# Second projection of a feed-forward block by rows of tokens instead of by columns of features

## The chip, the cores and the metric

The kernel runs on one core of a Trainium2 chip. The metric is device time in microseconds (us) of one execution, from the first to the last instruction of the core and what lies around it. Five engines work side by side, each through its own queue, in order: PE (TensorE, matrix products; its weight loads are shown apart as PEld), DVE (VectorE), ACT (ScalarE), POOL (GpSimd) and SP (SyncE, which here issues most DMAs).

## The reference

One layer of a streaming encoder for 2048 prompt tokens and 64 sample tokens, in float32. A mixer (windowed attention and a gated MLP) gives `mix`; then

```
h = layernorm(ALPHA * x + mix) * ln1_g + ln1_b          # 2112 x 1024
gu = h @ w_gate_up                                      # 1024 x 5632
f = (silu(gu[:, :2816]) * gu[:, 2816:]) @ w_down        # 2816 x 1024
y = layernorm(ALPHA * h + f) * ln2_g + ln2_b            # returned
```

with ALPHA = 2 ** 0.25. The change lies in how `h` is left behind by the first norm and in the last two lines. The mixer is as it was, up to the output projection.

## The kernel before

**Products.** Each operand of a product is split into two rounded terms (`split`: ACT copies the rounded term, DVE or POOL subtracts it to get the rest), and a product is three matmuls, high by high, high by low and low by high (`mm3`, lines 146 to 148, and lines 754 to 756). In a matmul one operand of 128 columns is loaded into the array (the stationary one) and the other streams through it (the moving one); "128x264" in a profile row is the moving operand.

**Output projection and first norm** (lines 584 to 653). Tile by tile of 128 tokens (17 tiles, the last of 64): `m2_load`, `m2_split`, `m2_mm` (48 matmuls of 512 columns, PSUM name `po`), `m2_add`, `m2_ln` (the norm without gain and shift, on DVE), `m2_T` (eight transposes on PE, then ACT multiplies by `ln1_g` and adds `ln1_b`, which lie along the partitions now) and a DMA of `h` by features, transposed, to `h_d` in DRAM.

**Feed-forward.** The 2112 tokens are cut into four blocks of 528. In a block, for each of 22 tiles of the hidden dimension, gate and up projections take seven products of half a block's tokens instead of eight (Strassen's scheme; `product`, 12 matmuls of 264 columns each, PSUM names `accA`, `accB`, `accC`). The weights' sums are made on POOL (`sums`, and line 732), and each weight form is split by ACT and by DVE or POOL (`form`, PSUM-free, two SBUF operands, 512 columns). The block's activations are loaded and their sums made and split in `prep_steps`, around the end of the block ahead of it: eight subtractions on POOL (line 671), fourteen splits on DVE (`hf`).

**Second projection.** Every two hidden tiles, `down` adds their products to y. y is kept by features: `yT` is eight tiles of 128 features by 528 tokens. `w_down` is stationary, `ff` is moving, 264 tokens at a time, so a pair of hidden tiles takes 16 calls of six matmuls (PSUM name `pd`) and 16 additions on DVE (line 1097). At the end of a block each `yT` tile goes to DRAM (`spill_y`), and the next block's start value is loaded from `h_d` (`new_y`). In the middle of the next block `finish_steps` fetches y in pieces of 106 tokens (`yf`), turns them by transposes on PE (`yTp`, eight for a piece, 15 pieces), and does the last norm: statistics, `norm` on ACT, `gain` on DVE (two operations), `shift` on POOL (two operations), DMA out. In the last block `z_old` turns the five pieces from SBUF (40 transposes) and the last two hidden tiles are multiplied by rows (`z_mm`, PSUM name `zp`: here `ff` is stationary and 512 columns of `w_down` move).

**Order.** All of it is written out by hand. `order` lists the products, 154 to a block; a product's place in it is called a position here. `make` builds weight forms five positions ahead. `at(pos, f)` puts every other piece of work behind the product at a position. For a pair of hidden tiles c, `p0` is the position of the product 3 of its second tile; for a block's last pair, p0 is the block's last position. Each engine runs its part of this list in order.

Of the kernel before, what the change touches and what calls it, by code (L numbers as in the profile page):

```python
# [35 lines left out]
PARTS = [[(106 * i, min(106, TB - 106 * i)) for i in range(5)]] * 3 + [[(116 * i, min(116, TB - 116 * i)) for i in range(5)]]  # L36
# [7 lines left out]
def hybrid_step(ctx: ExitStack, tc: tile.TileContext, x_prompt, x_sample, xT_prompt, xT_sample, cache_kT, cache_v, w_in,  # L44
# [14 lines left out]
    dram = ctx.enter_context(tc.tile_pool(name="dram", bufs=1, space=DRAM))  # L59
    wpool = ExitStack()  # L60
# [3 lines left out]
    y_d = [dram.tile([P, KD, TB], F32, name=f"y_d{b}") for b in range(NB - 1)]  # L64
    h_d = [dram.tile([P, KD, TB], F32, name=f"h_d{b}") for b in range(NB)]
# [76 lines left out]
    def mm3(out, parts):  # L142
        """out = sum of a^T b over parts, each an exact sum of two rounded terms"""
# [15 lines left out]
    def go(f, *a):  # L159
        """the next part of a step of the mixer"""  # L160
# [15 lines left out]
    def split_v(t, src, m):  # L176
        """a tile's values: per group the rounded term, then the rest"""
# [8 lines left out]
    def do_B(t):  # L186
# [7 lines left out]
        # rotary embedding of the first 16 dimensions of each head  # L194
# [38 lines left out]
    def split_k(t, cols, src):  # L233
        """a tile's keys in two terms, each on both halves of the partitions"""
# [86 lines left out]
    def spans(t):  # L321
        """columns of the scores of the even and the odd chunk of a tile"""
# [80 lines left out]
    def dup_v(t):  # L403
        """the values of a tile's first chunk and of the second one before it, each on both halves of the partitions"""
# [6 lines left out]
    def attn_PV(t, g):  # L411
        """the values' two terms lie side by side, so that the products of both come at once"""
# [57 lines left out]
    # constants of the mixer  # L470
# [32 lines left out]
    # a row of the first chunk doesn't see the second  # L503
# [61 lines left out]
    # weights of the output projection  # L565
# [54 lines left out]
    def m2_ln(t):  # L620
# [9 lines left out]
        nc.vector.tensor_scalar(tt[:m], tt[:m], mv[:m, 0:1], rs[:m], op0=ALU.subtract, op1=ALU.mult)  # L630

    def m2_T(t):
# [5 lines left out]
        for h in range(2):  # L638
# [20 lines left out]
    def prep_steps(b):
        """steps that bring a block's activations, and their sums, into the products' operands"""  # L660
        t = {}

        def load(key, kk, kh, sh):
            t[key, kk] = f1.tile([P, 2, NH], F32, name="hraw", tag="hraw", bufs=4)
            k0 = 4 * kh + 2 * kk
            nc.sync.dma_start(out=t[key, kk], in_=h_d[b][:, k0:k0 + 2, sh * NH:(sh + 1) * NH])

        def sub(out, x, y, kk):
            if (out, kk) not in t:
                t[out, kk] = f1.tile([P, 2, NH], F32, name="hsum", tag="hsum", bufs=2)  # L670
            nc.gpsimd.tensor_tensor(out=t[out, kk], in0=t[x, kk], in1=t[y, kk], op=ALU.subtract)

        def put(prod, key, kk):
            if kk == 0:
                forms[b, prod] = f1.tile([P, 2, 4, NH], F32R, name=f"hf{prod}", tag=f"hf{prod}", bufs=1)
# [3 lines left out]
        # each step with the position before the end of the block ahead after which it may come  # L679
# [26 lines left out]
    def slab_piece():  # L706
        return f1.tile([P, 4, P], F32, name="wsum", tag="hraw", bufs=4)
# [717 lines left out]
```

## Time and profile before

| | us |
|---|---|
| median of 3 runs (2229.14 to 2234.25) | 2230.99 |
| span of the profiled execution | 2229.8 |
| PE busy in the span | 2123.0 |
| DVE, ACT, POOL busy | 1756.9, 1147.4, 1026.5 |

The profiled execution's time is its span and about 1.2 us around it, if it is taken as the median run. Matmuls overlap in the array, so a busy PE says only that one was under way; how fast they follow each other is read from their start times. In rows of a timeline the columns are start, duration (us), engine, line, operation, output and inputs, shape, count, and in brackets the engine's idle time ahead of it and what ended it. Rows of windows give the length of each stretch, then the busy time of each engine with its instructions, then the mean granted TensorE clock (1.00 is 2.4 GHz, 0.50 is 1.2 GHz), the DMA share and GB/s.

### The profile page before, as it was taken

Reading aid. Unit: us, or ns where it says so; the run is one execution under the profiler, and the core shown is the slowest. Engines: PE = TensorE matmul, PEld = TensorE weight load, DVE = VectorE, ACT = ScalarE, POOL = GpSimd, SP = SyncE. Lnnn points to the kernel's source line nnn. Section 1 sums busy time; section 2 is a strip of 40 time slices with the busy share of each in tenths; the row PEclk is TensorE's granted clock in tenths of the full one; section 3 lists DMA queues with packets and bytes.
Section 4 is the critical chain, followed back from the end, with each engine's and each line's share of the span. In section 5 each row is a group of like instructions: output and inputs, shape, how many; then the busy total and the mean of one; then the engine's idle time right before and its main releaser. Section 6 shows DMA issues by size and latency. Waiting matters only on the chain.

```text
span 2229.8 us, 40289 instructions
## 1 busy us (share of the span) xinstructions
PE 2123.0 (95%) x15307; PEld 1996.7 (90%) x15307; DVE 1756.9 (79%) x3511; ACT 1147.4 (51%) x2675; POOL 1026.5 (46%) x813
## 2 busy tenths in 40 slices
PE   8999999989998999998999999899999989999995
PEld 6888888868887999998998999899999989999994
DVE  6877777786777877778777887877788787778876
ACT  6666656565565444445444444444444444444443
POOL 0222222230114646456555665656565656556642
PEclk9999999989999999999999999999999999999998
DMA  5111111134545332333533333353243335333321
GB/s 194 39 39 39 39 39 44 37 125 154 190 135 168 101 105 91 105 119 101 168 105 114 113 111 112 120 163 115 91 136 93 121 116 161 114 99 125 106 77 39
DMA packets 134096, 237.60 MB, mean 107 GB/s; under 512 B 36334, under 2 KB 59118, under 8 KB 133902
## 3 DMA queue, kind: packets, MB, share of 16 engines
q1 hardware_dynamic: 112638, 225.00, 31.5%
q10 hardware_dynamic: 21088, 9.70, 1.6%
q8 instruction: 120, 1.97, 0.3%
q14 instruction: 74, 0.61, 0.1%
q0 software_dynamic: 176, 0.33, 0.0%
HBM read 202.22 MB, written 32.77 MB: 105 GB/s over the span
## 4 chain that ended last, share of the span: by engine, by line
PE 55%; DVE 28%; ACT 8%; DMA 4%; issue 4%; POOL 0%; SPq 0%; ACTq 0%; DVEq 0%; POOLq 0%
DVE wf L101 6%; PE accA L755 5%; PE pd L146 5%; PE pd L147 5%; PE accA L754 5%; PE pd L148 5%; PE accA L756 5%; DMA yf<-y_d 3%; DVE yT L1097 3%; PE po L146 3%; PE po L147 3%; PE po L148 3%; DVE wd L101 3%; PE accC L755 2%; PE accC L756 2%
## 5 line engine op out<-in xcount | busy, mean ns | idle before, releaser
L146 PE MATMUL pd<-ff,wd 128*128 128x264 f32 x1376 | 398.8, 290 | 26.8 <-DVE yT L1097 25.4
L754 PE MATMUL accA<-hf,wf 128*128 128x264 f32 x1408 | 403.6, 287 | 7.7 <-ACT a L760 6.0
L756 PE MATMUL accA<-hf,wf 128*128 128x264 f32 x1408 | 402.9, 286 | 3.1 <-POOL wf L101 2.0
L755 PE MATMUL accA<-hf,wf 128*128 128x264 f32 x1408 | 404.7, 287 | 0.0
L147 PE MATMUL pd<-ff,wd 128*128 128x264 f32 x1376 | 393.6, 286 | 0.4 <-DVE ff L101 0.4
L148 PE MATMUL pd<-ff,wd 128*128 128x264 f32 x1376 | 392.9, 286 | 0.0
L101 DVE TENSOR_TENSOR wf<-wsum,wf 128x512 fp32r<-128x512 f32 x351 | 302.5, 863 | 28.4 <-ACT wf L100 28.3
L732 POOL TENSOR_TENSOR wsum<-guraw,wsum 128x512 f32<-128x512 f32 x87 | 114.1, 1311 | 443.9 <-DVE wf L101 432.7
L101 POOL TENSOR_TENSOR wf<-guraw,wf 128x512 fp32r<-128x512 f32 x173 | 267.9, 1549 | 70.3 <-ACT wf L100 66.6
L1097 DVE TENSOR_TENSOR yT<-pd,yT 128x264 f32<-128x264 f32 x624 | 252.1, 422 | 56.1 <-PE pd L148 56.1
L146 PEld LDWEIGHTS pd<-ff,wd 128*128 128x128 f32 x1376 | 261.0, 190 | 34.7 <-DVE yT L1097 34.5
L754 PEld LDWEIGHTS accA<-hf,wf 128*128 128x128 f32 x1408 | 268.8, 191 | 8.9 <-ACT a L760 6.9
L723 POOL TENSOR_TENSOR wsum<-guraw 128x512 f32<-128x512 f32 x176 | 269.3, 1530 | 15.1 <-PE accA L756 7.0
L756 PEld LDWEIGHTS accA<-hf,wf 128*128 128x128 f32 x1408 | 268.4, 191 | 3.6 <-POOL wf L101 2.2
L755 PEld LDWEIGHTS accA<-hf,wf 128*128 128x128 f32 x1408 | 269.0, 191 | 0.0
L147 PEld LDWEIGHTS pd<-ff,wd 128*128 128x128 f32 x1376 | 260.6, 189 | 0.6 <-DVE ff L101 0.6
L148 PEld LDWEIGHTS pd<-ff,wd 128*128 128x128 f32 x1376 | 260.3, 189 | 0.0
L100 ACT CAST ff<-c 128x264 fp32r<-128x264 f32 x176 | 72.7, 413 | 312.4 <-DVE c L767 312.4
L101 DVE TENSOR_TENSOR wd<-draw,wd 128x512 fp32r<-128x512 f32 x176 | 201.0, 1145 | 25.0 <-ACT wd L100 22.7
L100 ACT CAST wf<-wsum 128x512 fp32r<-128x512 f32 x351 | 216.4, 617 | 0.7 <-POOL wsum L723 0.5
L755 PE MATMUL accC<-hf,wf 128*128 128x264 f32 x704 | 201.3, 286 | 1.8 <-DVE hf L101 1.8
L754 PE MATMUL accC<-hf,wf 128*128 128x264 f32 x704 | 200.1, 284 | 1.3 <-DVE c L779 1.3
(285 smaller groups left out, 5424.4 us busy)
## 6 DMA issues: line engine op xcount, KB each, us to landing
guraw<-in_w_gate_up_dram SPq DMA_DIRECT2D x176, 512.0 KB, 4.2
draw<-in_w_down_dram SPq DMA_DIRECT2D x176, 256.0 KB, 4.5
hraw<-h_d SPq DMA_DIRECT2D x32, 264.0 KB, 4.2
yT<-h_d SPq DMA_DIRECT2D x32, 264.0 KB, 2.7
x<-in_xT_prompt_dram SPq DMA_DIRECT2D x32, 256.0 KB, 4.4
catx<-cat_d SPq DMA_DIRECT2D x16, 512.0 KB, 3.6
catx<-in_x_prompt_dram SPq DMA_DIRECT2D x16, 512.0 KB, 5.9
h_d<-catx ACTq DMA_DIRECT2D x13, 512.0 KB
```

Of the source, the lines that this page charges most:

```text
L100: nc.scalar.copy(hi, src)
L101: (on or nc.vector).tensor_tensor(out=lo, in0=src, in1=hi.bitcast(F32), op=ALU.subtract)
L146: nc.tensor.matmul(out, ah, bh, start=(i == 0), stop=False)
L147: nc.tensor.matmul(out, ah, bl, start=False, stop=False)
L148: nc.tensor.matmul(out, al, bh, start=False, stop=(i == n - 1))
L723: nc.gpsimd.tensor_tensor(out=src[key], in0=src[x], in1=src[y], op=op)
L732: nc.gpsimd.tensor_tensor(out=s4, in0=gu_src[b, i][2], in1=src, op=ALU.subtract)
L754: nc.tensor.matmul(ps, wh, hh, start=(new and k == 0), stop=False, skip_group_check=not new)
L755: nc.tensor.matmul(ps, wh, hl, start=False, stop=False, skip_group_check=not new)
L756: nc.tensor.matmul(ps, wl, hh, start=False, stop=(k == 3), skip_group_check=not new)
L1097: nc.vector.tensor_tensor(out=y, in0=pd[:, :NH], in1=y, op=ALU.add)
```

## The change

The second projection is turned round. `ff` is stationary, 128 tokens at a time, and 512 columns of `w_down` move, so the products come out as rows of tokens. Blocks are 512, 512, 512 and 576 tokens, which are 4, 4, 4 and 5 whole tiles (the fifth has 64 tokens). y stays in SBUF as rows, five tiles of 128 by 1024; nothing of it goes to DRAM and back, and no transposes are left in the last norm. The start value is no longer read from `h_d`: `m2_ln` now applies gain and shift itself (both times ALPHA, spread over the partitions once by `m2_gains`), its rows go to DRAM as `hy_d`, and `m2_T`'s ACT step only takes ALPHA off again. The last norm of a block runs beside the last pair's products instead of in the middle of the next block. Buffers: weight forms 7 for 8, sums 3 for 4, raw `w_down` 3 for 4; the sum for product 7 is made later; products add in place; the second hidden tile's weights are loaded later, and the first tile's form 3 is built from its sources.

```diff
-TB = TOK // NB
-NH = TB // 2
+TB = (512, 512, 512, 576)
+TILES = tuple(tuple(range(4 * b, 4 * b + (5 if b == NB - 1 else 4))) for b in range(NB))
...
     def m2_ln(t):
...
-        nc.vector.tensor_scalar(tt[:m], tt[:m], mv[:m, 0:1], rs[:m], op0=ALU.subtract, op1=ALU.mult)
+        nc.vector.scalar_tensor_tensor(out=tt[:m], in0=tt[:m], scalar=mv[:m, 0:1], in1=gb_t[0][:m], op0=ALU.subtract, op1=ALU.mult)
+        nc.vector.scalar_tensor_tensor(out=tt[:m], in0=tt[:m], scalar=rs[:m], in1=gb_t[1][:m], op0=ALU.mult, op1=ALU.add)
+    def m2_gains():
+        for v in range(2):
+            gb_t[v] = f1.tile([P, KD, P], F32, name="gb", tag="raw", bufs=4).rearrange("p k q -> p (k q)")
+            for h in range(2):
+                pt = ps1.tile([P, 4, P], F32, name="gbp", tag="pj")
+                for j in range(4):
+                    c = 16 + 8 * v + 4 * h + j
+                    nc.tensor.transpose(pt[:, j], vecT[:, c:c + 1].to_broadcast([P, P]), ident)
+                nc.scalar.activation(gb_t[v][:, h * 512:(h + 1) * 512], pt.rearrange("p j q -> p (j q)"), AF.Copy, scale=ALPHA)
...
     def m2_T(t):
...
-            for j in range(4):
-                k = 4 * h + j
-                nc.scalar.activation(hT[:, k, :m], pt[:, j, :m], AF.Identity, scale=vecT[:, 16 + k:17 + k],
-                                     bias=vecT[:, 24 + k:25 + k])
+            nc.scalar.activation(hT[:, 4 * h:4 * h + 4, :m], pt[:, :, :m], AF.Copy, scale=1.0 / ALPHA)
...
+        nc.scalar.dma_start(out=h_d[b][:, :, o:o + m], in_=hT[:, :, :m])
+        nc.scalar.dma_start(out=hy_d[t][:m], in_=tt[:m])
...
-    m2_ln(0)
     go(gate_T, 16)
...
+    m2_gains()
     for t in range(NT - 4):
...
-        if t:
-            m2_ln(t)
+        m2_ln(t)
...
-        if t in (NT - 10, NT - 7):
-            load_gu(0, (t - NT + 10) // 3)
+        if t == NT - 10:
+            load_gu(0, 0)
...
     m2_ln(16)
-    make(EARLY)
+    load_gu(0, 1)
     product(*order[0])
...
-    def down(b, c, j, s):
+    def down(b, c, t, h, last=False):
...
-        mm3(pd[:, :NH], [((wd[b, i, j // 4][:, 0, js], wd[b, i, j // 4][:, 1, js]), (ff[b, i][:, 0, sl], ff[b, i][:, 1, sl]))
-                         for i in (2 * c, 2 * c + 1)])
+        mm3(pd[:m], [((ff[b, i][:, 0, o:o + m], ff[b, i][:, 1, o:o + m]), (wd[b, i, h][:, 0], wd[b, i, h][:, 1]))
+                     for i in (2 * c, 2 * c + 1)])
+        y = y_t[t][:m, h * 512:(h + 1) * 512]
+        nc.vector.tensor_tensor(out=y, in0=pd[:m], in1=y, op=ALU.add)
+    def new_y(t):
+        m = rows(t)
+        y_t[t] = f2.tile([P, D], F32, name="y", tag="y", bufs=5)
+        nc.sync.dma_start(out=y_t[t][:m], in_=hy_d[t][:m])
...
-        if b:
-            for k, e in enumerate(PARTS[b - 1]):
-                for q, f in enumerate(finish_steps(b - 1, *e)):
-                    at(first + (39, 53, 66, 81, 95)[k] + (0, 2, 3, 5, 5, 7, 7, 8)[q], f)
...
+            if c < NFF // 2 - 1:
+                where = (2, 3, 4, 5, 7, 8, 9, 10, 12, 13) if last else (2, 4, 5, 7, 9, 10, 12, 13)
+                for k, (h, t) in enumerate((h, t) for h in range(2) for t in TILES[b]):
+                    at(p0 + where[k], lambda b=b, c=c, t=t, h=h: down(b, c, t, h))
+            elif not last:
+                new = list(TILES[b + 1])
+                at(p0 + 3, lambda t=new.pop(0): new_y(t))
+                for k, t in enumerate(TILES[b]):
+                    for h in range(2):
+                        at(p0 + (6, 7, 8, 9, 10, 11, 12, 13)[2 * k + h], lambda b=b, c=c, t=t, h=h: down(b, c, t, h))
+                    steps = finish_steps(t)
+                    for q, f in zip((7, 8, 9, 10, 11), steps):
+                        at(p0 + 2 * k + q, f)
+                    at(p0 + 2 * k + 13, lambda t=new.pop(0): new_y(t)) if new else None
```

The five steps of `finish_steps(t)` are now: statistics of the first half; of the second half, and their moments (with the reciprocal root on POOL); `norm`, one ACT operation over 1024 columns; `gain`, two DVE operations; `shift`, two POOL operations and one DMA out. `z_mm` and what follows it keep their order and work on the rows in place.

## Rows read from the trace of the kernel before

**Rows 1.** The page's first part: busy time of the engines, share of the span, instructions.

```profile
PE 2123.0 (95%) x15307; PEld 1996.7 (90%) x15307; DVE 1756.9 (79%) x3511; ACT 1147.4 (51%) x2675; POOL 1026.5 (46%) x813
```

**Rows 2.** Stretches of the feed-forward part: the three ends of a block (55 us each) and the three stretches between them (250 us each).

```profile
1015.00:1070.00 55.00, 47.54 (x359) 46.24 (x359) 49.22 (x76) 25.64 (x54) 34.74 (x23) 0.94 0.35 110
1400.00:1455.00 55.00, 46.74 (x359) 45.25 (x358) 49.12 (x77) 25.65 (x54) 34.42 (x22) 0.97 0.36 111
1785.00:1840.00 55.00, 46.10 (x355) 44.58 (x354) 48.47 (x76) 26.57 (x56) 31.61 (x21) 0.97 0.37 116
1070.00:1320.00 250.00, 240.52 (x1938) 238.02 (x1938) 196.80 (x352) 118.94 (x251) 145.56 (x101) 0.99 0.40 124
1455.00:1705.00 250.00, 240.90 (x1951) 238.44 (x1951) 198.38 (x352) 119.65 (x253) 148.10 (x102) 0.99 0.40 124
1840.00:2090.00 250.00, 240.70 (x1949) 238.22 (x1948) 198.62 (x352) 119.40 (x252) 150.26 (x104) 0.99 0.40 124
```

**Rows 3.** What PE waited for from 640 us on: total us, times, longest.

```profile
PE pd L146 <- DVE yT L1097: 25.4, 21, 3.9
PE yTp L1140 <- DMA yf<-y_d: 16.3, 9, 3.4
```

**Rows 4.** Timeline of PE: first and last of 81 matmuls of 264 columns in a row, of 23 of 256 columns, of 19 of 512 columns in the output projection (`po`), and of 59 of 512 columns in the last products by rows (`zp`); then eight transposes and the matmul after them.

```profile
1399.75 0.28 PE L754 MATMUL accA<-hf,wf 128*128 128x264 f32 x1
...
1409.50 0.29 PE L756 MATMUL accB<-hf,wf 128*128 128x264 f32 x1
...
282.28 0.28 PE L147 MATMUL pj<-wB0l,xh 128*128 128x256 f32 x1
...
284.78 0.28 PE L148 MATMUL pj<-wB0h,xl 128*128 128x256 f32 x1
...
559.81 0.39 PE L148 MATMUL po<-wo01h,cathl 128*128 128x512 f32 x1
...
563.89 0.39 PE L148 MATMUL po<-wo11h,cathl 128*128 128x512 f32 x1
...
2190.04 0.40 PE L1183 MATMUL zp<-wd,ff 128*116 128x512 f32 x1
...
2203.51 0.40 PE L1184 MATMUL zp<-wd,ff 128*64 128x512 f32 x1
...
564.12 1.03 PE L642 MATMUL hTp<-ident,catx 128*128 128x128 f32 x8
564.91 0.48 PE L146 MATMUL po<-wo00h,cathl 128*128 128x512 f32 x1
```

**Rows 5.** Timeline of PE around the longest wait in the middle of a block.

```profile
1211.96 1.07 PE L1140 MATMUL yTp<-ident,yf 128*106 128x128 f32 x4 [3.37 <-DMA yf<-y_d]
...
1213.05 0.42 PE L147 MATMUL pd<-ff,wd 128*128 128x264 f32 x1
1213.27 0.42 PE L148 MATMUL pd<-ff,wd 128*128 128x264 f32 x1
```

**Rows 6.** Timeline of DVE and of POOL at the end of the second block: the same DVE operation alone and beside POOL, one that reads PSUM, and POOL's operations at that time.

```profile
1409.05 0.68 DVE L101 TENSOR_TENSOR wf<-wsum,wf 128x512 fp32r<-128x512 f32 x1
...
1416.22 1.81 DVE L101 TENSOR_TENSOR wf<-wsum,wf 128x512 fp32r<-128x512 f32 x1
1417.96 0.42 DVE L779 TENSOR_TENSOR c<-accC,a 128x264 f32<-128x264 f32 x1
...
1414.45 1.30 POOL L671 TENSOR_TENSOR hraw<-hraw 128x528 f32<-128x528 f32 x1
1415.70 1.78 POOL L671 TENSOR_TENSOR hsum<-hraw,hsum 128x528 f32<-128x528 f32 x1
```

**Rows 7.** DVE's groups of instructions from 1400 to 1455 us that have two operands in SBUF: busy us, mean ns of one, idle time ahead.

```profile
L101 DVE TENSOR_TENSOR wf<-wsum,wf 128x512 fp32r<-128x512 f32 x11 | 10.9, 991 | 0.0
...
L101 DVE TENSOR_TENSOR hf<-hraw,hf 128x528 fp32r<-128x528 f32 x8 | 7.6, 950 | 0.0
L101 DVE TENSOR_TENSOR wd<-draw,wd 128x512 fp32r<-128x512 f32 x5 | 7.3, 1452 | 1.4 <-ACT wd L100 1.4
L101 DVE TENSOR_TENSOR hf<-hsum,hf 128x528 fp32r<-128x528 f32 x6 | 5.6, 938 | 0.0
...
L101 DVE TENSOR_TENSOR wf<-guraw,wf 128x512 fp32r<-128x512 f32 x3 | 3.2, 1057 | 0.0
```

**Rows 8.** DVE's groups over the whole span: an addition out of PSUM of 512 columns, and the gain and the statistics of the last norm.

```profile
L618 DVE TENSOR_TENSOR catx<-po,catx 128x512 f32<-128x512 f32 x32 | 22.1, 692 | 14.9 <-PE po L148 13.0
...
L1152 DVE TENSOR_TENSOR z<-z,ln2g 106x512 f32<-106x512 f32 x24 | 16.6, 692 | 12.2 <-ACT z L1148 12.1
L1117 DVE BATCH_NORM_STATS2 yst<-z 106x6 f32<-106x512 f32 x24 | 16.4, 684 | 0.0
```

**Rows 9.** Timelines where the output projection becomes the only work: ACT's and PE's start on tile 2, and DVE's normalisation of a tile; then two stretches, the output projection's end and the passage to the feed-forward part.

```profile
505.55 2.46 ACT L601 ACTIVATE cathl<-catx,vecT 128x128 fp32r<-128x128 f32 x8 [3.31 <-DMA catx<-cat_d]
...
506.01 0.50 PE L146 MATMUL po<-wo00h,cathl 128*128 128x512 f32 x1
...
520.27 0.82 DVE L630 TENSOR_SCALAR catx<-catx,hmv,hrs 128x1024 f32<-128x1024 f32 x1 [0.73 <-POOL hrs L80]
...
600.00:680.00 80.00, 80.00 (x381) 64.67 (x380) 65.33 (x123) 49.10 (x132) 17.62 (x17) 1.00 0.40 119
680.00:725.00 45.00, 39.42 (x287) 37.23 (x286) 32.59 (x44) 24.60 (x59) 23.36 (x17) 0.92 0.63 200
```

More of the change, by code (lines that the diff above doesn't have):

```diff
@@ L59, in hybrid_step @@
     dram = ctx.enter_context(tc.tile_pool(name="dram", bufs=1, space=DRAM))
+    const.tile([P, 24], F32, name="pad")
+    edge = ctx.enter_context(tc.tile_pool(name="edge", bufs=1, side="right"))
+    edge.tile([P, 24], F32, name="edge")
     wpool = ExitStack()
@@ L63, in hybrid_step @@
     cat_d = [dram.tile([P, KD, P], F32, name=f"cat_d{t}") for t in range(NT)]
-    y_d = [dram.tile([P, KD, TB], F32, name=f"y_d{b}") for b in range(NB - 1)]
-    h_d = [dram.tile([P, KD, TB], F32, name=f"h_d{b}") for b in range(NB)]
+    h_d = [dram.tile([P, KD, TB[b]], F32, name=f"h_d{b}") for b in range(NB)]
+    hy_d = [dram.tile([P, D], F32, name=f"hy_d{t}") for t in range(NT)]
     ident = const.tile([P, P], F32, name="ident")
@@ L674, in put @@
             if kk == 0:
[L675 removed]
+                forms[b, prod] = f1.tile([P, 8 * NHX], F32R, name=f"hf{prod}", tag=f"hf{prod}", bufs=1)[:, :8 * n].rearrange(
+                    "p (s k t) -> p s k t", s=2, k=4)
             o = forms[b, prod][:, :, 2 * kk:2 * kk + 2]
@@ L762, in add @@
         def add(key, to):
-            part[i, key] = tmp(key)
-            nc.vector.tensor_tensor(out=part[i, key][:, :n], in0=ps, in1=part.pop((i, to))[:, :n] if to != "a2" else part[i, to][:, :n], op=ALU.add)
+            part[i, key] = a = part.pop((i, to))
+            nc.vector.tensor_tensor(out=a[:, :n], in0=ps, in1=a[:, :n], op=ALU.add)
         def out(sh, g, u):
@@ L776, in product @@
             keep("a2")
-            c = acc[i, "C"][:, :n]
-            part[i, "c22"] = tmp("c22")
-            nc.vector.tensor_tensor(out=part[i, "c22"][:, :n], in0=c, in1=part.pop((i, "a2"))[:, :n], op=ALU.add)
+            part[i, "c22"] = a = part.pop((i, "a2"))
+            nc.vector.tensor_tensor(out=a[:, :n], in0=acc[i, "C"][:, :n], in1=a[:, :n], op=ALU.add)
         elif prod == 2:
@@ L812, in make @@
                 if made > EARLY:
-                    sums(b, i)
+                    sums(b, i, (5, 6) if i else (5, 6, 7))
             form(b, i, p)
             if made == EARLY:
-                sums(0, 1)
+                sums(0, 1, (5, 6))
             made += 1
             if p == 3:
+                if (b, i + 1) in gu_src and 7 not in gu_src[b, i + 1]:
+                    sums(b, i + 1, (7,))
                 nx = b * NFF + i + 2
@@ L1145, in norm, with finish_steps, z @@
+    def finish_steps(t):
+        s_, m = {}, rows(t)
+        def z(h):
+            return y_t[t][:, h * 512:(h + 1) * 512]
         def norm():
             shift_of(s_, m)
-            for h in range(2):
-                nc.scalar.activation(z[h][:m], z[h][:m], AF.Identity, scale=s_["rs"][:m, 0:1], bias=s_["rs"][:m, 1:2])
+            nc.scalar.activation(y_t[t][:m], y_t[t][:m], AF.Identity, scale=s_["rs"][:m, 0:1], bias=s_["rs"][:m, 1:2])
         def gain():
             for h in range(2):
-                nc.vector.tensor_tensor(out=z[h][:m], in0=z[h][:m], in1=ln2g[:m, h * 512:(h + 1) * 512], op=ALU.mult)
+                nc.vector.tensor_tensor(out=z(h)[:m], in0=z(h)[:m], in1=ln2g[:m, h * 512:(h + 1) * 512], op=ALU.mult)
@@ L1154, in shift @@
         def shift():
             for h in range(2):
-                nc.gpsimd.tensor_tensor(out=z[h][:m], in0=z[h][:m], in1=ln2b[:m, h * 512:(h + 1) * 512], op=ALU.add)
-                nc.sync.dma_start(out=y_rows(b, o, m, h), in_=z[h][:m])
-        return [fetch, lambda: rows_of(0), lambda: (rows_of(1), stats(s_, z, m, 0)), lambda: stats(s_, z, m, 1),
-                lambda: moments(s_, m), norm, gain, shift]
+                nc.gpsimd.tensor_tensor(out=z(h)[:m], in0=z(h)[:m], in1=ln2b[:m, h * 512:(h + 1) * 512], op=ALU.add)
@@ L1164, in hybrid_step @@
+            nc.sync.dma_start(out=y_out(t), in_=y_t.pop(t)[:m])
+        return [lambda: stats(s_, (z(0), z(1)), m, 0), lambda: (stats(s_, (z(0), z(1)), m, 1), moments(s_, m)), norm, gain, shift]
     zs, zp, zm = {}, {}, {}
-    def z_old(k, h):
-        o, m = PARTS[NB - 1][k]
-        pt = ps1.tile([P, 512], F32, name="yTp", tag="pj")
-        for j in range(4):
-            nc.tensor.transpose(pt[:m, j * P:(j + 1) * P], yT[4 * h + j][:, o:o + m], ident)
-        zs[k, h] = (f1.tile([P, 2 * NH], F32, name="z", **({"tag": "hraw", "bufs": 4} if k < 2 else {"tag": "hsum", "bufs": 2}))[:, :512]
-                    if k < 3 else f2.tile([P, 512], F32, name="z", tag="draw", bufs=4))
-        nc.scalar.copy(zs[k, h][:m], pt[:m])
@@ L1175, in z_mm @@
     def z_mm(k, h, i):
-        o, m = PARTS[NB - 1][k]
+        t = TILES[-1][k]
+        m, o = rows(t), k * P
         i += NFF - 2
@@ L1186, in z_add @@
     def z_add(k, h):
-        m = PARTS[NB - 1][k][1]
+        m = rows(TILES[-1][k])
         z = zs[k, h]
@@ L1201, in z_sum @@
     def z_sum(k, h):
-        m = PARTS[NB - 1][k][1]
+        m = rows(TILES[-1][k])
         if h == 0:
@@ L1207, in z_mean @@
     def z_mean(k):
-        m = PARTS[NB - 1][k][1]
+        m = rows(TILES[-1][k])
         sm, mv = zm[k]["sum"], zm[k]["mv"]
```

128 lines of the change are left out of this document (49 added, 79 removed).

## The prediction

> **What bounds the kernel now.** I read the page's first part, then stretches, PE's waits, start times of matmuls, and last what DVE and POOL do where PE waits. PE is under way for 95% of the span [rows 1], so what counts is how fast matmuls follow each other and the little time in which none runs. The stretches show where that is. At each end of a block PE is idle for 7.5, 8.3 and 8.9 us of 55, and for some 9.3 us in each 250 us between [rows 2]. Two waits stand out: for DVE's additions to y (25.4 us) and for pieces of y from DRAM before the transposes (16.3 us) [rows 3]. A wait costs more than itself: after the one of 3.37 us, matmuls of 264 columns start every 0.22 us, against 0.122 [rows 4, 5], which is the clock's lower level of 1.2 GHz for a while.
>
> Why a block's end is slow is seen on DVE and POOL. The same subtraction of 128x512 takes 0.68 us on DVE alone and 1.81 beside POOL; one that reads PSUM keeps its 0.42 [rows 6]. So DVE's operations with two SBUF operands and POOL's take turns. Their own times, without the waiting, add up at the end of the second block: fourteen `wf` by 0.68, fourteen `hf` by 0.70 (528 columns), five `wd` by 0.69, nine narrower ones (splits of `ff`, a product in `c`) by 0.42, together 26.8 us [rows 6, 7]; 22 operations on POOL by 1.30 [rows 2, 6], 28.6 us. That is 55.4 of 55 us: this turn-taking, not PE, sets the pace there.
>
> The Trainium skill has this as a rule (SBUF — State Buffer, section Who interferes with whom): a DVE instruction with two SBUF inputs and a GpSimd instruction that reads SBUF block each other fully. The trace agrees, 0.68 against 1.81 us.
>
> **The parts of the change.** The sum is made against the profiled execution, span 2229.8 us and 1.2 around it.
>
> *Products of gate and up.* 7392 matmuls; in blocks 0 to 2 they move 256 columns instead of 264 (5544 of them), in block 3 288 (1848). Before: 9.75 us over 80 steps, 0.1219 each [rows 4], 901.1 us. For 256 columns the bounds are 0.1136 (2.50 us over 22 steps, in the mixer [rows 4]) and 0.1182 (0.1219 by columns); the feed-forward part seems a little slower than the mixer, so I take 0.116, and for 288 likewise 0.1305 (0.1278 to 0.1330). 643.1 + 241.2 = 884.3: **-16.8** (-35 to 0).
>
> *Second projection.* Before, 43 pairs of hidden tiles by 96 matmuls of 264 columns: 4128 x 0.1219 = 503.2. After, 33 pairs by 48 and 10 by 60 (the half tile streams all 512 columns): 2184 of 512 columns. Bounds are 0.2267 (`po`, 4.08 us over 18 steps) and 0.2322 (`zp`, 13.47 over 58) [rows 4]; `zp` has the same operands, so 0.2315: 505.6, **+2.4** (-8 to +4). Fewer matmuls, but no fewer columns.
>
> *Transposes.* 120 in `finish_steps` and 40 in `z_old` go. Eight take 0.79 us [rows 4]: 160 x 0.099 = **-15.8**. Their ACT copies were not waited for and give nothing.
>
> *The middle of the blocks.* The idle 9.5, 9.1 and 9.3 us [rows 2] come from fetched pieces and from DVE at the last norm; that norm moves away, so **-27.9**. With it goes the lower clock, 0.01 of 250 us three times, **-7.5**. What is left there still takes turns: for one hidden tile (7 positions) six POOL operations by 1.30 and on DVE five `wf`, two `wd` and four narrow ones, 6.0 us, make 13.8, while PE needs 7 x 12 x 0.116 + 5.6 = 15.3. PE stays the bound there, at 90%. Spills and fetches of y leave SP's queue; the rows `hy_d` are written from ACT's queue in the output projection and replace the loads from `h_d`, hidden under PE.
>
> *The ends of the blocks.* The last norm now falls on the stretch that was already paced by the turn-taking. I count 27 positions, from the first `hf` split (8 before the block's end) to 18 after it. Before: 27/7 x 13.8 = 53.2, `hf` 14 x 0.70 = 9.8, six subtractions 7.8, together 70.8; PE: 27 products by 1.463 and 29 calls of `down` by 0.731, 60.7. That is 10.1 too much, and lost were 24.7 us of idle PE and 6.6 of clock at the three ends [rows 2], 10.4 each: the count holds. After: the same 70.8, and for four tiles eight gains by 0.69 [rows 8] and eight shifts by 1.30, 15.9: 86.7. PE has less to do: 27 x 1.392 and 15 calls by 1.389, 58.4. Too much by 28.3. Weight forms are made five positions ahead, some 7 us of PE's work, which can soak up part, so I take 22, and 16 for the third end, where the next block's products and its fifth tile give PE 6 us more. 60 against 31.2: **+28.8** (0 to +48). Behind a late gain on DVE stand weight forms and the additions out of PSUM, and for these PE waits. On SP, `new_y` waits for the output of the tile whose buffer it takes, and loads of weights stand behind it; the first `down` on such a tile comes three to six positions after the load is issued (8 us or more), so this adds nothing unless POOL is late by more than that.
>
> *The output projection.* Tile 0's norm can't start until `m2_gains` has run: 16 transposes on PE (1.6 us) and four ACT copies. ACT waited here for a load until 505.55 and PE started tile 2 at 506.01 [rows 9]. Now ACT ends the gains at about 508, DVE the two wide operations at about 510.2, PE tile 0's transposes at about 511.3: 5.3 us, and some 3 us of lower clock after it, **+8.3** (1.6 to 9). Later `m2_ln` costs DVE twice 1.38 (two 512-column operations by 0.69 [rows 8]) for 0.82 [rows 9], about 1.9 more a tile; at 65.3 of 80 us busy [rows 9] and seven tiles it comes to 79, just fitting: **+2** (0 to 8). ACT's two wide copies for eight narrow ones are off the path.
>
> *Passage and tail.* The second hidden tile's weights come later, the form 3 costs three POOL operations for one, and some buffers go; but PE is idle here for 5.6 us anyway [rows 9], with the same engines late: 0 (-3 to +5). The end behind `z_mm` keeps its chain: 0.
>
> Sum: -16.8 + 2.4 - 15.8 - 27.9 - 7.5 + 28.8 + 8.3 + 2 = -26.5. 2229.8 - 26.5 + 1.2 = 2204.5, so **2205**.
>
> **Rivals.** *Slower: the block's end eats more than the middle gives.* If nothing is absorbed and DVE's other work there isn't covered by POOL's turns either (15 additions by 0.69, 8 statistics by 0.68, some 6.5 us of products' additions, 22.4; half of it 11.2), an end costs 39.5 and the third 33.5: 112.5, 52 more, 2257. It decides from about 29 for each end, where the gain is used up. For it: DVE runs its list in order and was busy 49 of 55 us there [rows 2]. Against: before, the plain count came out right. By the rule of the SBUF page a blocked engine waits for the whole instruction of the other; worked out with the rows' times, that is the full 28.3 at two ends and 22 at the third, and the sum would be 2223.
>
> *Faster: the ends cost what they did,* since the extra work sinks into the lead, and 256 columns run at 0.1136: -28.8 and -18, 2158. For it: at 90% the turn-taking has room right behind the stretch. Against: 28 us is four times the lead.
>
> *No change.* The idle time only moves from the middle of a block to its end: the ends take 22 us more than I say in sum, and the pitch stays by columns, within 4.5 us of 2231.
>
> **The numbers.** Forecast (2175 to 2226) 0.51, slower 0.21, faster still 0.15, no change 0.13. A measurement can tell about 0.2%, 4.5 us, from no change. So faster 0.66, same 0.13, slower 0.21. Slow pitches and late ends reach 2245, quick ones 2170; that leaves out the slower case beyond it and the quickest.
>
> **What would show it.** The stretches between the ends without idle PE and without `yTp`; start times of `pd` 0.227 to 0.232 apart, of products of 256 columns 0.114 to 0.118; at each end some 22 us of idle PE, most of it behind DVE additions and `wf` splits, with DVE's SBUF operations at two to three times their 0.69 and POOL over 80% busy; PE's start on tile 2 some 5 us later. It is wrong if the ends lose 30 us or more each, if PE waits for `y` loads there, or if matmuls of 256 columns don't start faster than by columns.

## The result and the profile after

The changed kernel takes 2249.18 us (median; 2248.67 to 2250.62) beside 2230.06 for the kernel before on the same chip: ratio 1.0084, 95% interval 1.0070 to 1.0098. It is slower by 0.8%; the forecast was 2205 (2175 to 2226 for its own case, 2170 to 2245 in all). The profiled span is 2246.8 us against 2229.8. The page's first part, answering [rows 1]:

```profile
PE 2132.8 (95%) x13219; PEld 1907.6 (85%) x13219; DVE 1774.0 (79%) x3183; ACT 1086.0 (48%) x2519; POOL 986.0 (44%) x806
```

The order of the products is the same in both kernels (88 hidden tiles by 7, 154 in a block). So I compare the start of the product at a given position of that order. Worked out from the matmuls' start times, in us; the last three columns belong to the experiments ("norm in the middle" is the run at the better places, and the last one adds form 3's new source to it):

| stage, by positions | before | changed | without the pads | norm in the middle | and form 3 |
|---|---|---|---|---|---|
| until the first product | 682.0 | 690.6 | 690.4 | 691.9 | 691.0 |
| passage, 0 to 20 | 43.6 | 50.2 | 49.9 | 51.1 | 48.0 |
| block 0, 20 to 148 | 293.5 | 286.5 | 280.2 | 280.2 | 280.2 |
| first end, 148 to 178 | 80.8 | 95.5 | 97.6 | 79.5 | 79.4 |
| block 1, 178 to 302 | 303.2 | 278.0 | 271.8 | 272.1 | 273.5 |
| second end, 302 to 332 | 80.9 | 96.7 | 97.2 | 80.1 | 80.1 |
| block 2, 332 to 456 | 301.7 | 278.0 | 271.8 | 272.1 | 272.1 |
| third end, 456 to 486 | 81.4 | 99.0 | 99.9 | 88.1 | 88.2 |
| block 3, 486 to 615 | 320.2 | 333.5 | 332.7 | 332.7 | 332.7 |
| rest of the span | 42.5 | 38.7 | 38.7 | 39.0 | 39.1 |

The middles of blocks 1 and 2 gain 24 to 25 us each, and the three ends give back 48. The stretches show it, first the second end in the kernel before (its 30 positions), then the three ends after and two stretches in the middle. Columns: stretch, length, busy PE, PEld, DVE, ACT, POOL with instructions, granted clock, DMA share, GB/s.

```profile
1403.10:1484.00 80.90, 72.64 (x572) 71.15 (x572) 69.42 (x112) 39.69 (x85) 48.93 (x33) 0.98 0.46 146
```

```profile
1027.30:1122.80 95.50, 78.71 (x464) 70.38 (x463) 82.66 (x117) 41.69 (x84) 60.35 (x44) 0.87 0.36 122
1400.80:1497.50 96.70, 76.58 (x464) 68.31 (x463) 83.71 (x119) 42.68 (x87) 60.18 (x44) 0.88 0.35 120
1775.40:1874.50 99.10, 83.57 (x476) 74.81 (x475) 86.41 (x120) 43.97 (x87) 62.06 (x44) 0.90 0.37 121
...
1130.00:1370.00 240.00, 240.00 (x1657) 223.45 (x1656) 194.52 (x277) 111.17 (x244) 131.22 (x95) 1.00 0.33 104
1515.00:1755.00 240.00, 240.00 (x1653) 223.20 (x1653) 191.62 (x276) 112.35 (x247) 127.11 (x92) 1.00 0.33 106
```

In the middle PE has no idle time and the full clock, where [rows 2] had 9.3 us idle and 0.99. At the ends it is idle for 16.8, 20.1 and 15.5 us and runs at 0.87 to 0.90. At the second end DVE is busy for 14 us more than before, POOL for 11. PE's waits from 1015 to 2100 us (total, times, longest), answering [rows 3], and ACT's at the second end:

```profile
PE accA L779 <- ACT a L785: 33.9, 14, 4.6
PE pd L150 <- ACT wd L104: 8.6, 3, 4.1
PE pd L151 <- DVE wd L105: 8.2, 6, 2.3
```

```profile
ACT ff L104 <- DVE a L792: 16.4, 9, 4.1
ACT a L807 <- DVE a L789: 15.9, 4, 4.8
ACT a L814 <- DVE a L789: 10.4, 5, 3.5
ACT y L1157 <- DVE yrs L1142: 10.0, 4, 5.2
```

`yT` and `yf` are gone from the list. PE now waits for ACT to copy a product (`a`) before it goes on in that bank. ACT is no bottleneck by its busy share (44% at the ends); it works through its list in order and stands at operations whose input DVE has not finished.

### The profile page after: what moved, and what is told of

Same layout as the page of the kernel before. It is cut to its first block, busy times and chain, and to the rows that moved or that the text cites. A ratio compares the mean times of both kernels' runs of the same rounds, so it can differ in the third digit from the quotient of the medians.

```text
span 2246.8 us, 35596 instructions
## 1 busy us (share of the span) xinstructions
PE 2132.8 (95%) x13219; PEld 1907.6 (85%) x13219; DVE 1774.0 (79%) x3183; ACT 1086.0 (48%) x2519; POOL 986.0 (44%) x806
## 4 chain that ended last, share of the span: by engine, by line
PE 67%; DVE 22%; ACT 5%; issue 4%; POOL 1%; DMA 1%; SPq 0%; ACTq 0%; DVEq 0%; POOLq 0%
PE accA L779 6%; PE pd L151 6%; PE pd L150 6%; PE pd L152 6%; PE accA L781 6%; PE accA L780 6%; PE accC L779 3%; PE accC L781 3%; PE accC L780 3%; DVE wf L105 3%; PE pj L150 2%; PE pj L151 2%; PE pj L152 2%; PE po L150 2%; PE po L152 2%
## 5 line engine op out<-in xcount | busy, mean ns | idle before, releaser
L779 PE MATMUL accA<-hf,wf 128*128 128x256 f32 (+1 forms) x1408 | 412.2, 293 | 41.5 <-ACT a L785 37.4
L781 PE MATMUL accA<-hf,wf 128*128 128x256 f32 (+1 forms) x1408 | 408.9, 290 | 1.1 <-DVE wf L105 1.1
L780 PE MATMUL accA<-hf,wf 128*128 128x256 f32 (+1 forms) x1408 | 407.0, 289 | 0.8 <-DVE hf L105 0.8
L744 POOL TENSOR_TENSOR wsum<-guraw 128x512 f32<-128x512 f32 x176 | 252.5, 1435 | 304.3 <-DVE wf L105 304.3
L105 DVE TENSOR_TENSOR wf<-wsum,wf 128x512 fp32r<-128x512 f32 x352 | 342.3, 973 | 40.8 <-ACT wf L104 40.2
L779 PEld LDWEIGHTS accA<-hf,wf 128*128 128x128 f32 x1408 | 270.5, 192 | 56.1 <-ACT a L785 43.6
L1120 DVE TENSOR_TENSOR y<-pd,y 128x512 f32<-128x512 f32 (+1 forms) x364 | 248.6, 683 | 84.7 <-PE pd L152 84.3
L150 PE MATMUL pd<-wd,ff 128*128 128x512 f32 (+1 forms) x728 | 290.8, 399 | 8.6 <-ACT wd L104 8.6
L151 PE MATMUL pd<-wd,ff 128*128 128x512 f32 (+1 forms) x728 | 290.6, 399 | 8.2 <-DVE wd L105 8.2
L152 PE MATMUL pd<-wd,ff 128*128 128x512 f32 (+1 forms) x728 | 288.3, 396 | 0.0
L780 PEld LDWEIGHTS accA<-hf,wf 128*128 128x128 f32 x1408 | 271.8, 193 | 9.6 <-DVE hf L105 1.2
L105 DVE TENSOR_TENSOR wd<-draw,wd 128x512 fp32r<-128x512 f32 x176 | 213.4, 1212 | 26.1 <-ACT wd L104 22.8
L104 ACT CAST ff<-a 128x256 fp32r<-128x256 f32 (+1 forms) x176 | 72.7, 413 | 301.0 <-DVE a L792 301.0
L779 PE MATMUL accC<-hf,wf 128*128 128x256 f32 (+1 forms) x704 | 203.6, 289 | 0.0
L781 PE MATMUL accC<-hf,wf 128*128 128x256 f32 (+1 forms) x704 | 202.8, 288 | 0.0
L780 PE MATMUL accC<-hf,wf 128*128 128x256 f32 (+1 forms) x704 | 201.7, 287 | 0.0
L105 DVE TENSOR_TENSOR ff<-a,ff 128x256 fp32r<-128x256 f32 (+1 forms) x176 | 115.3, 655 | 84.4 <-ACT ff L104 84.4
L152 PEld LDWEIGHTS pd<-wd,ff 128*128 128x128 f32 (+1 forms) x728 | 136.0, 187 | 34.9
```

The costliest lines, as they stand in the source:

```text
L104: nc.scalar.copy(hi, src)
L105: (on or nc.vector).tensor_tensor(out=lo, in0=src, in1=hi.bitcast(F32), op=ALU.subtract)
L150: nc.tensor.matmul(out, ah, bh, start=(i == 0), stop=False)
L151: nc.tensor.matmul(out, ah, bl, start=False, stop=False)
L152: nc.tensor.matmul(out, al, bh, start=False, stop=(i == n - 1))
L779: nc.tensor.matmul(ps, wh, hh, start=(new and k == 0), stop=False, skip_group_check=not new)
```

## The experiments

**The place of the tiles.** Matmuls of 256 columns started 0.120 us apart and not 0.116; in the mixer, whose code is the same, pitches had moved too. What was common was the two unused tiles of 96 bytes, `pad` and `edge` (with a pool of its own). They belong to the change, though the cut of its diff above doesn't show them.

```
-    const.tile([P, 24], F32, name="pad")
...
-    edge.tile([P, 24], F32, name="edge")
```

> The changed kernel without its two unused tiles of 96 bytes (`pad`, `edge`), so that all tiles lie again 32 bytes off a multiple of 64, as in the kernel before. Theory A (the pitch of matmuls hangs on where the operands lie): matmuls of 256 columns in the feed-forward part start 0.113 to 0.117 us apart and not 0.120, those of 288 at 0.130 and not 0.133, those of 512 in the mixer at 0.233 and not 0.227; 5544 x 0.005 + 1848 x 0.003 less, 1224 x 0.006 more: 2249 becomes about 2223 (2215 to 2230). Rival (the pitch is that of the columns and of the feed-forward part's operands, the place does nothing): pitches unchanged, 2249 within 4.

2232.36 us, 0.9999 (0.9990 to 1.0009) of the kernel before: the pads cost 17 us. That is a little less than theory A's range, as 256 columns fell to 0.1176 and not to 0.113 to 0.117. By the table of stages the pads cost 6 us in each of blocks 0 to 2, while the ends are 0.5 to 2 us shorter with them, which fits ends whose pace PE doesn't set. First and last of 36 matmuls in a row, then first and last of six of `pd`, with the pads and without:

```profile
1195.47 0.28 PE L779 MATMUL accC<-hf,wf 128*128 128x256 f32 x1
...
1199.67 0.28 PE L781 MATMUL accA<-hf,wf 128*128 128x256 f32 x1
1199.79 0.40 PE L150 MATMUL pd<-wd,ff 128*128 128x512 f32 x1
...
1200.96 0.40 PE L152 MATMUL pd<-wd,ff 128*128 128x512 f32 x1
```

```profile
1189.10 0.28 PE L776 MATMUL accC<-hf,wf 128*128 128x256 f32 x1
...
1193.23 0.28 PE L778 MATMUL accA<-hf,wf 128*128 128x256 f32 x1
1193.34 0.39 PE L147 MATMUL pd<-wd,ff 128*128 128x512 f32 x1
...
1194.48 0.39 PE L149 MATMUL pd<-wd,ff 128*128 128x512 f32 x1
```

4.20 us over 35 steps became 4.13, 1.17 over 5 became 1.14. The same pads in the kernel before:

> The kernel before with the two unused tiles of 96 bytes of the changed kernel, so that its tiles lie at multiples of 64 bytes. Theory A (place): in the mixer matmuls of 256 columns start 0.120 apart and not 0.1136 (408 of them, +2.7 us), those of 512 at 0.227 and not 0.233 (1224, -7 us); those of 264 at 0.122 to 0.1235 (11520, 0 to +17 us): 2231 becomes 2226 to 2244. Rival (place does nothing): all pitches as before, 2231 within 4.

2232.3 us, 1.0003 (0.9993 to 1.0012). The mixer's pitches moved as theory A says (table); those of 264 columns by only 0.0005, and the time lies within the ranges of both theories. The expectation has the places wrong here: worked out from the addresses that the pools give, the feed-forward part of the kernel before has `hf` 32 bytes off a multiple of 64, but `wf` and `ff` at multiples; with the pads it is the other way round. So this run compares the two mixed places, in which matmuls of 256 columns turn out alike (next table). Then one pad at a time:

> The changed kernel without the unused tile `edge` alone: the tiles of the right side (weight forms, `ff`, `wd`, y) lie 32 bytes off a multiple of 64, those of the left side (`hf`) at multiples of 64. If it is the stationary operand's place (weight forms and `ff` are stationary): products of 256 columns 0.1176 apart as without both tiles, `pd` 0.2278. If it is the moving operand's (`hf` left, `wd` right): products stay at 0.120, `pd` goes to 0.2278.

> The changed kernel without the unused tile `pad` alone: the left side's tiles (`hf`) lie 32 bytes off a multiple of 64, the right side's (weight forms, `ff`, `wd`) at multiples of 64, the other way round than in the run without `edge`. If only the right side's place counts: products of 256 columns at 0.120 and `pd` at 0.2325, as in the changed kernel. If the left side's counts too (without `edge` products took 0.1168, without both 0.1176): products of 256 columns at 0.120 to 0.121; `pd`, whose operands all lie on the right, at 0.2325.

2234.7 and 2233.6 us, one time each. Mean pitch of matmuls that follow without a gap, ns (places from the addresses, as above):

| off a multiple of 64, left / right side | 256, products | 288, products | 512, `pd` | 256, mixer | 512, mixer (`pj`) |
|---|---|---|---|---|---|
| 0 / 0 (changed) | 119.9 | 133.0 | 232.5 | 120.0 | 230.5 |
| 32 / 32 (no pads) | 117.6 | 132.4 | 227.8 | 115.5 | 234.5 |
| 0 / 32 (no `edge`) | 116.8 | 133.5 | 230.4 | 120.5 | 234.2 |
| 32 / 0 (no `pad`) | 116.8 | 133.5 | 230.5 | 120.5 | 234.1 |
| before (mixer 32 / 32); before with pads (0 / 0) | | | | 115.1; 120.0 | 234.3; 230.4 |

Both of my readings fall: either pad alone gives the same pitches, also for `pd`, whose operands all lie on the right. That the place matters is shown; that it is an operand's place is refuted for `pd`. The 512-column matmuls of the output projection (`po`) stay at 227 in all six kernels. By what way the place acts stays open.

**The last norm at a block's end.** All that follow stand without the pads, on 2232, unless said otherwise. First, with the pads, gain and shift left out (`gain`: `pass`; `shift`: the output alone), and the norm done by DVE alone (two `scalar_tensor_tensor` on each half for `norm`, `gain` and `shift`):

> The changed kernel without the two halves of `gain` and `shift` in the finish of blocks 0 to 2 (gain and shift of the last norm are left out there; statistics, `norm` and output stay). Theory B (DVE's and POOL's turns set the pace at the ends of the blocks): 15.9 us of turns go at each end, idle PE there falls by 12 to 16 us each, 2249 becomes about 2207 (2200 to 2215). Rival (ACT's queue: `norm` waits there for the statistics, and copies of products stand behind it): only 2 to 5 us each, 2235 to 2243.

> The changed kernel with the last norm of blocks 0 to 2 as two DVE operations on each half (minus mean times gain, times reciprocal deviation plus shift), nothing of it on ACT and only the power of one column on POOL. Theory B (turns): for a tile DVE 4 x 0.69 in place of 2 x 0.69 and POOL's 2 x 1.30, 1.2 us less, 5 for each end, 2249 becomes about 2234 (2228 to 2240). Rival (ACT's queue behind `norm`): the wait of ACT goes as a whole, 10 us or more at each end, 2219 or less.

2230.67 (0.9994, 0.9984 to 1.0004) and 2245.13 (1.0061, 1.0046 to 1.0076): some 6 and 1.5 us less at an end, not 12 to 16 and not 5. Both theories miss. So I took the norm out as a whole (`finish_steps` returns the output alone), then part by part:

> As the first experiment (the changed kernel without its unused tiles, 2232), and the finish of blocks 0 to 2 only writes y out: statistics, norm, gain and shift of the last norm are left out there. Theory C (the last norm as a whole does it: its 16 additions, statistics and narrow operations on DVE, and ACT's list, in which `norm` waits for DVE's result, 10 us at each end): the ends fall to what they were before, 81 us for 30 positions against 97 now; with PE's 2.3 us less work some 16 each, 2232 becomes about 2184 (2178 to 2192). Rival (something else of the change, the loads of `new_y` in SP's list or the closer `down` calls): ends stay above 88 us, 2205 or more.

> As the first experiment (2232), with `norm` left out of the finish of blocks 0 to 2 (ACT's operation over the row and the narrow one of DVE before it); statistics, gain, shift and output stay. Theory D (ACT's list: ACT stands still at `norm` for DVE's result, 10 us at each end, and the copies of products and weight forms stand behind it): each end 8 to 10 us shorter, about 2205 (2200 to 2209). Rival E (DVE's own work with its turns is what counts): 0 to 3 us each, 2223 to 2232.

> As the first experiment (2232), with the statistics left out of the finish of blocks 0 to 2 (eight 512-column operations of DVE for a block, the narrow ones behind them and POOL's power of one column); ACT's operation stays, with a constant factor, so that it waits for no statistics; gain, shift and output stay. Theory D: as without `norm`, 8 to 10 us for each end from ACT's list, and 2 to 4 more from DVE: 2190 to 2205. Rival E: eight by 0.69 and four sets of narrow ones by 0.5, 7.5 us of DVE's time for each end, 2210 (2207 to 2216).

> As the first experiment (2232), with POOL's shift alone left out of the finish of blocks 0 to 2 (eight operations by 1.30 at each end). Turns (each microsecond of POOL is one that DVE doesn't have): 10 us at each end, 2202 to 2212. Theory E (DVE's own time counts, POOL's operations fall into its gaps): 0 to 2 us each, 2226 to 2232.

> As the first experiment (2232), with DVE's gain alone left out of the finish of blocks 0 to 2 (eight operations by 0.69 at each end). Theory E: their own time, 5 to 6 us each, 2214 to 2217. Turns with POOL: the same or less, since POOL's shift stays. If gain and shift only matter together: 0 to 2 us each, 2226 to 2232.

The times, with what the first two ends took:

| left out of the finish | us | ratio to before | ends 1 and 2 |
|---|---|---|---|
| nothing | 2232.36 | 0.9999 (0.9990 to 1.0009) | 97.6, 97.2 |
| shift (POOL) | 2228.5 | 0.9988 (0.9978 to 0.9997) | 95.4, 96.0 |
| `norm` (ACT), with a DVE operation of one column | 2221.2 | 0.9952 (0.9935 to 0.9968) | 93.4, 93.1 |
| gain (DVE) | 2216.75 | 0.9932 (0.9917 to 0.9947) | 91.2, 90.6 |
| statistics (DVE), with POOL's power; `norm` waits for nothing | 2209.51 | 0.9899 (0.9884 to 0.9914) | 88.0, 87.9 |
| all | 2184.68 | 0.9792 (0.9778 to 0.9807) | 79.5, 79.0 |

Theory C holds with its number (2184): the whole norm is 18 us at each of the first two ends, and nothing else of the change lengthens these. At the third it is 13; what is left there, 87 us, is still 6 more than before, with more work for PE (78 us busy, 70 at the second). Of the norm's parts, POOL's 10.4 us of shifts (eight by 1.30) are worth 1 to 2, DVE's gain and statistics 6.5 and 9.5, ACT's `norm` 4. They add up to 22 and not 18, so they are not independent. Theory E has its range without shift, without gain and without statistics; without `norm`, 2221 lies between the ranges of D and E. The second end in the same order, all columns as above:

```profile
1389.90:1487.10 97.20, 76.66 (x464) 68.33 (x463) 83.90 (x119) 43.30 (x88) 61.07 (x44) 0.86 0.34 119
```

```profile
1387.20:1483.20 96.00, 75.11 (x463) 67.15 (x462) 82.40 (x121) 44.28 (x90) 50.37 (x36) 0.89 0.35 121
```

```profile
1386.20:1479.30 93.10, 75.50 (x463) 68.08 (x462) 84.05 (x113) 37.03 (x81) 62.42 (x44) 0.89 0.36 125
```

```profile
1385.20:1475.80 90.60, 74.05 (x463) 66.34 (x462) 77.26 (x111) 43.53 (x88) 60.53 (x44) 0.92 0.37 128
```

```profile
1382.90:1470.80 87.90, 72.48 (x463) 65.66 (x462) 77.00 (x96) 40.58 (x84) 60.81 (x40) 0.92 0.38 132
```

```profile
1372.80:1451.80 79.00, 69.77 (x463) 64.00 (x462) 67.87 (x93) 39.61 (x85) 46.96 (x32) 0.96 0.44 147
```

Read DVE's column against the length: the length is DVE's busy time and 11 to 14 us, also in the kernel before (69.42 of 80.90). That time includes what an operation of DVE waits for POOL inside it [rows 6]. POOL goes from 61 to 50 in the second row and the length hardly moves. Only the row without `norm` is shorter at the same DVE time, by 4 us, a fifth of the whole. Whether that is ACT's list (theory D) or the one-column operation of DVE that went with it isn't shown, and without statistics too ACT waits less, so not all of the 9.5 us there is DVE's. DVE's groups at the second end of the changed kernel (1408 to 1500 us; busy, mean ns of one, idle ahead) show what was added:

```profile
L105 DVE TENSOR_TENSOR wf<-wsum,wf 128x512 fp32r<-128x512 f32 x17 | 19.8, 1163 | 2.8 <-ACT wf L104 2.8
L1120 DVE TENSOR_TENSOR y<-pd,y 128x512 f32<-128x512 f32 x16 | 10.9, 679 | 0.0
...
L1161 DVE TENSOR_TENSOR y<-y,ln2g 128x512 f32<-128x512 f32 x8 | 7.3, 949 | 0.0
...
L1138 DVE BATCH_NORM_STATS2 yst<-y 128x6 f32<-128x512 f32 x8 | 5.4, 680 | 0.0
...
L1142 DVE SCALAR_TENSOR_TENSOR yrs<-ymv,yrs 128x1 f32<-128x1 f32 x4 | 3.5, 885 | 0.0
```

Gain, statistics and one operation of one column come to 16.2 us, about DVE's difference between the first and the last row (83.90 and 67.87).

**The norm back in the middle.** A finished tile of y goes to DRAM as rows and is normed in the next block, from two halves in the `hraw` buffers:

```
+    at(p0 + 2 * k + 8, lambda t=t: spill_y(t))
...
+    for k, t in enumerate(TILES[b - 1]):
+        for q, f in zip((0, 6, 7, 8, 10, 11, 12), finish_steps(t)):
+            at(first + 32 + 22 * k + q, f)
```

> As the first experiment (2232), but the last norm of blocks 0 to 2 is taken back to the middle of the next block: a finished tile of y goes to DRAM as rows, and is fetched in halves 32, 54, 76 and 98 positions into the next block, with no transposes. Theory C: the ends fall as in the run without the norm, by about 16 us each; in the middle its 4 tiles lie in DVE's and POOL's spare 10% and cost 0 to 3 us for each block: about 2188 (2180 to 2198). Rival (the middle has no room, and PE loses there what it lost before, 9 us for each block): 2205 to 2215.

> As the run before (last norm in the middle of the next block), and the last 8 `down` calls of a block come at the 12 positions of the other pairs (2 to 13 after the product 3) and not at 6 to 13. If PE waits at the ends because the calls come too close together: 2 to 5 us less for each end, 6 to 15 in all than the run with the norm alone moved. If not: the same within 4.

2208.5 (0.9900, 0.9883 to 0.9916) and 2209.43 (0.9901, 0.9886 to 0.9915). That is the rival's range and not theory C's 2188: the first two ends fall to 79.5 and 79.2 as in the run without the norm, but blocks 1 and 2 lose 11.5 us each, and block 3, with its 288 columns, nothing. In the second of these runs the ends are 1.4 us shorter and the blocks 2 to 3 longer, so the closer `down` calls are not it. Within a block the four tiles lost 1.9, 4.4, 0 and 5.2 us. So the next run moves only `32 + 22 * k` to `(34, 62, 76, 104)[k]`:

> The run with the last norm in the middle of the next block, its four tiles begun 34, 62, 76 and 104 positions into it and not 32, 54, 76 and 98, so that each lies in the pairs of hidden tiles as the third did, which cost PE nothing in that run, while the others cost 1.9, 4.4 and 5.2 us. If the place against the `down` calls is what costs: blocks 1 and 2 lose 0 to 2 us and not 10.7, about 2189 (2185 to 2193). Rival (there is no room for four tiles in a block wherever they lie): 2205 to 2212.

2187.82 (0.9802, 0.9787 to 0.9817), as the first reading has it. A stretch in the middle of block 1, at the first places and at the better ones:

```profile
1148.00:1320.00 172.00, 164.63 (x1136) 151.85 (x1137) 145.34 (x212) 79.85 (x176) 109.11 (x75) 0.99 0.35 118
```

```profile
1150.00:1322.00 172.00, 171.95 (x1210) 161.18 (x1209) 146.10 (x222) 84.65 (x184) 114.22 (x78) 1.00 0.36 123
```

DVE is as busy in both (145 and 146), but PE gets through 74 more matmuls in the second. So the place in the lists tells, and not the amount of work. That it is the meeting with `down` and its splits is how I chose the places, and isn't shown by itself.

**The passage.** It was forecast at 0 and cost 6.6 us.

> As the first experiment (2232), and the second hidden tile's gate and up weights are loaded some 130 us earlier: the norms of token tiles 13 to 16 take the tile itself in place of the gain and shift rows (gain and shift are wrong there), so that the two buffers of the rows come free. If the passage is longer by 7.7 us because these weights come late: 6 to 8 us of it go, 2225. If it is the three POOL operations for the form 3 and the fewer buffers: 0 to 2 us, 2231.

2230.53 (0.9991, 0.9982 to 1.0001); the first 12 products took 31.0 us against 31.2, so late weights are not it. POOL's waits from 670 to 725 us in the run without the pads name another: the form 3's source (`wsum`) lies in memory that the output projection gives back when its last rows have gone out. But in the run just shown the same operation waits nearly as long for PE, and the products are no quicker:

```profile
POOL wsum L756 <- DMA hy_d<-catx: 9.6, 1, 9.6
```

```profile
POOL wsum L756 <- PE accA L778: 8.4, 1, 8.4
```

With that source in an `hraw` buffer:

> The run with the last norm in the middle at the better places (2188), with the source of the first hidden tile's form 3 in a free tile of the left side (a buffer of the block's activations) and not in the memory that the output projection gives back. If the passage is longer because POOL waits 9.6 us there for that memory: its 12 products take 26 to 29 us and not 32.6, 2182 to 2185. If it is the three POOL operations for the form 3: 31 or more, 2186 to 2189.

2185.75 (0.9791, 0.9776 to 0.9805). POOL's waits from 670 to 730 us in the run before and in this one:

```profile
POOL wsum L757 <- DMA hy_d<-catx: 10.9, 1, 10.9
```

```profile
POOL wsum L742 <- DMA hy_d<-catx: 6.4, 1, 6.4
```

The wait of 10.9 us goes, one of 6.4 comes (for the next hidden tile's sums), and the 12 products take 29.5 us and not 32.6, beside 24.0 in the kernel before. Other kernels with the change took 31.0 to 33.1, so 1.5 to 3.6 of some 8 us are explained, and the rest stays open; the two medians, 2187.82 and 2185.75, are too close to tell it. This kernel keeps the change's rows, blocks and first norm. It has no pads, the last norm is back in the middle, with y written to DRAM and fetched, and form 3's source lies elsewhere. It is 2.1% faster than the one before.

## Why the prediction was wrong

- **Products of gate and up, forecast -16.8: failed.** The step took 0.116 and 0.1305 for 256 and 288 columns, "a little slower than the mixer". Measured: 0.1199 and 0.1330, beside 0.1216 for 264. 5544 x (0.1199 - 0.1216) + 1848 x (0.1330 - 0.1216) = +11.6 us, outside the bound of 0. The whole diff has both pads, and I gave them no term. Without them it is 0.1176 and 0.1324, -2.2 us: the mixer's pitch was no guide even then. So the pads are half of the 28 us by which this term is off; the other half is that, over the blocks of 256 and of 288 columns, the time stays nearly as the columns do. The sign that I named, 256 columns not faster than by columns, came true (0.1199 for 0.1182).
- **Second projection, +2.4:** `pd` at 0.2325 for 0.2315, 2184 x 0.2325 - 4128 x 0.1217 = +5.4 with the pads, a little outside its bounds, -4.9 without.
- **Transposes and the middle, -15.8 and -35.4: right.** No `yTp`, no idle time, clock 1.00.
- **Ends, +28.8: the direction was right, the price was not.** Idle time, and lost clock as its share of PE's busy time: 16.8 + 0.13 x 78.7, 20.1 + 0.12 x 76.6 and 15.5 + 0.10 x 83.6 are 27, 29 and 24, together 80 us for 60. Counted so, the 31.2 before are 30.3 (the forecast took the clock's share of all 55 us), so +50. Two steps failed.
  - "which can soak up part, so I take 22", and 16 at the third end: the forecast's own count was 28.3, 28.3 and 22, and 27, 29 and 24 came. Nothing of the 7 us of lead shows in them; taking them off makes 19 of the 20 us that the ends' 60 is short of.
  - The count itself, "eight gains by 0.69 [rows 8] and eight shifts by 1.30, 15.9". It put POOL's time on the path and left out the statistics, the narrow operations and ACT's wait. The runs show the opposite shares, so that 15.9 lies near the 18 measured is luck. That the count came to 55.4 of 55 us before was no proof of it: DVE's busy time alone was 49 of those 55. Its sums slip, too: the four kinds of DVE operation add up to 26.6 and not 26.8, and the 6.0 us of DVE for a hidden tile are 6.5 if a narrow operation takes 0.42 as it does ahead; then 11.9 us were too much before, and not 10.1 beside 10.4.
  - The signs I named say so too: POOL was to be over 80% busy (60 of 96, 63%), PE to wait for DVE's additions (it waited for ACT's copies), DVE's operations to take two to three times 0.69 (gains took 0.95, `wf` splits 1.16).
- The Trainium skill (SBUF — State Buffer, section Who interferes with whom) has a DVE instruction with two SBUF inputs contend with a GpSimd instruction that reads SBUF. The single operations agree (0.68 alone, 1.81 beside POOL [rows 6]). As a price for the stretch POOL's time doesn't hold: without 10.4 us of shifts an end is 1 to 2 us shorter.
- **Output projection, +10.3:** it took +8.6. Its steps came within a microsecond: gains ready at 508.8 (forecast 508), DVE done at 510.4 (510.2), PE on tile 2 at 512.07, 6.1 us later than in [rows 9] (5.3):

```profile
507.75 1.09 ACT L649 ACTIVATE gb<-gbp 128x512 f32<-128x512 f32 x2 [0.25 <-PE gbp L648]
...
509.12 1.28 DVE L636 SCALAR_TENSOR_TENSOR catx<-catx,hrs,gb 128x1024 f32<-128x1024 f32 x1
...
512.07 0.78 PE L150 MATMUL po<-wo00h,cathl 128*128 128x512 f32 x1
```

- **Passage, 0 (-3 to +5):** +6.6. "PE is idle here for 5.6 us anyway" hid a new wait of POOL for memory, which explains 1.5 to 3.6 us; the rest is open. **Tail, 0:** -3.8.

The measured terms make +27 and the spans differ by 17. Where the other 10 lie isn't shown; 1 of them is counted twice, as 9 of the transposes lay in the tail. Of the rivals, the full count without the lead, 78.6 us at the ends and 2223 in all, came nearest to the measured 80; the slower one had 112 there, so that its 2257 lies near 2249 is luck, made up for by the products. Both put POOL's shifts at their full time, which the runs don't bear out. Against the forecast's 2205 the products are 28 us too high, the ends 21, the passage 7 and the second projection 3; the tail and the output projection give back 5, and with the 10 that can't be placed this is the difference of 44.

## What to carry to other kernels

Where several engines work in order, price added work by the one whose busy time follows the length of the stretch, with all its operations, and check that by taking out one engine's part: here a norm with 16 us of work on DVE cost 18 us at an end, and its 10 us on POOL alone were worth 1 to 2. Work that must be done somewhere belongs where that engine has room, and there at places where its list isn't needed at once: moved so, the same norm cost some 1 us a block (2187.8 beside 2184.7 without it) and not 13 to 18. An unused tile that shifts all addresses is an edit with a price of its own, and is worth a run by itself.

## What the runs showed of the hardware

- A shift of all tiles by 96 bytes, 32 modulo 64, changed the pitch of matmuls of the same shape by up to 5 ns: 115 to 120 for 256 columns and 234 to 230 for 512 (`pj`) in the mixer, 228 to 232 for `pd`; `po` stayed at 227. The better place isn't the same for all of them, and the other side's place counts even where no operand lies there.
- Matmuls of 264 columns took 121.6 ns with one side off a multiple of 64. By columns 256 would take 117.9; they took 116.8 with one side off, 117.6 with both off and 119.9 with neither.
- A DVE operation of a single column took 0.885 us on average beside POOL's work [as `yrs` above], and 0.69 in the run without POOL's shifts.
